# A new order for the 35 DMA transfers of a matmul-and-subtract kernel

## Chip, cores, metric

One core of one Trainium2 chip. The time is device microseconds of one execution; the span in a profile is some 1.8 us shorter than the time of the same run (1.7 to 1.9 us in every run on record). Chips differ little here, but a few runs are up to 3 us longer. Runs over 1.5% above the fastest are called slow and are left out of the verdicts.

The words used below: a transfer is issued when the sync engine's DMA instruction starts, and has landed when its semaphore says that all of its rows are in place. The stream is what the 16 DMA engines move one after another; a hole is a time in which they have nothing queued. The head is the part of the kernel before the steady loop.

## The reference

```python
# x: 16 x 512 x 1024, weight: 1024 x 768, sub_value: 16 x 512 x 768, all float32
def reference(x, weight, sub_value):
    return (np.matmul(x, weight) - sub_value).astype(np.float32)
```

In the kernel, rows are taken in 64 m tiles of 128. Traffic is 33.6 MB of x, 3.1 MB of weight, 25.2 MB of sub_value and 25.2 MB of output: 87.03 MB in all.

## The kernel before

ScalarE casts x to f16. Forty tiles are transposed on TensorE and copied out of PSUM (the memory that TensorE writes) by ScalarE, 24 (in pairs) on VectorE. Each tile then has 16 matmuls of 384 columns. VectorE subtracts, in place in the ring that held sub_value, and the ring's slots are stored. All DMA is issued by the sync engine from one list, in order. An entry is (what, first tile, number of tiles); w counts chunks of 256 rows of the weight:

```python
NX, NSO = 16, 32          # slots of the x ring and of the sub_value/output ring
TRANSFERS = [
    ('x', 0, 1), ('w', 0, 1), ('x', 1, 1), ('w', 1, 1), ('x', 2, 2), ('w', 2, 1),
    ('w', 3, 1), ('x', 4, 4), ('s', 0, 5), ('x', 8, 8), ('s', 5, 3), ('s', 8, 8),
    ...
]
```

An entry waits for what its slots held before; entries behind it wait too (cut from the kernel, comments added):

```python
old = {t - NX if kind == "x" else t - NSO for t in span}
need, by = {
    "w": (set(), "o"),
    "x": ({t for t in old if t >= 0}, "cast"),     # the cast has read the slot
    "s": ({t for t in old if t >= 0}, "o"),        # the store has landed
    "o": (span, "finish"),                         # the subtraction is done
}[kind]
```

The steady loop, cut to its order:

```python
for mi in range(HEAD, n_mt):
    tr = transposes(mi + TA) ...          # unless that pair goes to VectorE
    for c in range(n_c):
        matmuls(mi, c)
        if tr:
            tr[c]()
    ...                                   # casts of later tiles, on ScalarE
    finish(mi)                            # the subtraction, on VectorE
    for f in waiting[:PER]:               # six transpose pieces on VectorE
        f()
```

## Time and profile before

| | kernel before |
|---|---|
| time, first three runs | 211.04 us median (210.6 to 211.05) |
| span of the profiled run | 208.5 us (time of this run 210.34 us) |
| TensorE busy | 195.9 us, 94% |
| DMA queue | 98.0% of 16 engines, 87.03 MB |
| last subtraction ends / last store issued / landed | 203.20 / 203.23 / 207.26 us |

A busy share says that an engine had work, not that it set the end: two rows near 100% can both be read as the bound. The prediction shows the lines. One more line, from the list of DMA issues (size of each, median us from issue to landing), is that of the last two stores:

```profile
out_dram<-so_ring SPq DMA_DIRECT2D x2, 384.0 KB, 4.8
```

A store of 384 KB takes 0.90 us of all engines at their rate; 4.8 us is latency or a queue ahead of it. Which of the two, the profile of this kernel alone doesn't tell.

### The profile page before, as it was taken

To read this page: it belongs to the slowest core of one execution; us is meant where nothing else is said; L and a number is where in the kernel's file an instruction comes from. 1 tells how busy PE (TensorE), PEld (TensorE's weight loads), DVE (VectorE), ACT (ScalarE), POOL (GpSimd) and SP (SyncE) were. 2 spreads that over 40 slices of the span, in tenths; PEclk is the share of its full clock that TensorE was granted. 3 is DMA by queue.
4 is the path that set the end of the run, shared out by engine and by line. 5 is a ranking of instruction groups with operands and counts; after the bars stand their busy time and mean duration, and the time that the engine had idled before them with its cause. 6 is when DMAs were issued, how large, how long until landed. Compare 5 with 4: busy or idle time off the path is not lost.

```text
span 208.5 us, 2449 instructions
## 1 busy us (share of the span) xinstructions
PE 195.9 (94%) x1216; PEld 75.7 (36%) x704; DVE 147.4 (71%) x266; ACT 103.1 (49%) x105; POOL 0.7 (0%) x6
## 2 busy tenths in 40 slices
PE   7959879999999999999999999999999999999970
PEld 2413434443343434343434333343434343344420
DVE  0231043369999999998899969999999999423330
ACT  2640556976446371916463275537291821467400
POOL 1000000000000000000000000000000000000000
PEclk9996999999999999999999999999999999999998
DMA  6999999999999999999999999999999999999994
GB/s 198 424 437 425 458 437 383 457 405 438 433 445 429 439 421 422 442 429 420 408 463 431 417 430 442 445 386 430 434 426 447 424 431 434 443 446 395 460 390 199
DMA packets 4906, 87.17 MB, mean 418 GB/s; under 512 B 544, under 2 KB 544, under 8 KB 1568
## 3 DMA queue, kind: packets, MB, share of 16 engines
q1 hardware_dynamic: 4896, 87.03, 98.0%
q8 instruction: 7, 0.11, 0.2%
q14 instruction: 3, 0.02, 0.0%
HBM read 61.87 MB, written 25.17 MB: 417 GB/s over the span
## 4 chain that ended last, share of the span: by engine, by line
PE 88%; DMA 5%; ACT 1%; SPq 1%; DVE 1%; issue 0%
PE po_b L180 79%; PE pt_b L317 8%; DMA so_ring<-in_weight_dram 5%; ACT xt_b L324 1%; PE po_b L405 1%; SPq L280 1%; DVE w_sb L247 0%; DVE so_ring L388 0%; ACT x_b L299 0%; SPq L244 0%; SPq L517 0%; SPq L134 0%
## 5 line engine op out<-in xcount | busy, mean ns | idle before, releaser
L180 PE MATMUL po_b<-w_sb,xt_b 128*128 128x384 f16 x640 | 113.3, 329 | 3.5 <-DVE w_sb L247 2.6
L344 DVE STREAM_TRANSPOSE xtp_b<-x16p_b 32x256 f32<-32x256 f32 x192 | 83.6, 435 | 8.2 <-ACT x16p_b L299 5.2
L388 DVE TENSOR_TENSOR so_ring<-po_b,so_ring 128x768 f32<-128x768 f32 x64 | 60.0, 956 | 34.7 <-PE po_b L180 21.6
L324 ACT COPY xt_b<-pt_b 128x1024 f16<-128x1024 f16 x40 | 40.4, 1012 | 81.4 <-PE pt_b L317 81.0
L180 PE MATMUL po_b<-w_sb,xtp_b 128*128 128x384 f16 x384 | 73.6, 326 | 0.0
L368 PEld LDWEIGHTS <-xt_b 128*128 128x128 f16 x320 | 31.7, 99 | 63.2 <-issue 60.3
L299 ACT CAST x_b<-x_ring 128x1024 f16<-128x1024 f32 x40 | 41.5, 1045 | 8.8 <-DMA x_ring<-in_x_dram 8.7
L317 PE MATMUL pt_b<-ident,x_b 128*128 128x128 f32 x160 | 41.1, 273 | 1.3 <-ACT x_b L299 1.3
L317 PEld LDWEIGHTS pt_b<-ident,x_b 128*128 128x128 f32 x160 | 22.0, 141 | 34.8 <-issue 31.6
L299 ACT CAST x16p_b<-x_ring 128x1024 f16<-128x1024 f32 x24 | 25.1, 1046 | 3.9 <-DMA x_ring<-in_x_dram 3.8
L368 PEld LDWEIGHTS <-xtp_b 128*128 128x128 f16 x192 | 18.8, 98 | 21.9 <-issue 20.1
L247 DVE CAST w_sb<-so_ring 128x768 f16<-128x768 f32 x8 | 4.1, 557 | 11.8 <-DMA so_ring<-in_weight_dram 11.8
L405 PE MATMUL po_b<-idle_x,idle_w 128*128 128x512 f16 x31 | 9.3, 454 | 1.5 <-DVE idle_x L399 1.5
L405 PEld LDWEIGHTS po_b<-idle_x,idle_w 128*128 128x128 f16 x31 | 3.5, 114 | 5.9 <-issue 2.7
L299 ACT ACT_TABLE_LOAD x1 | 1.3, 1283 | 0.9 <-SPq L134 0.9
L398 DVE MEMSET idle_w<- 128x64 uint32 x1 | 0.1, 112 | 1.0 <-SPq L134 1.0
L418 PE MATMUL po_b<-idle_x,idle_w 128*128 128x512 f16 x1 | 0.4, 379 | 0.0
L169 POOL TENSOR_SCALAR_AFFINE_SELECT ident<-ident 128x128 f32<-128x128 f32 x1 | 0.3, 292 | 0.1
L399 DVE MEMSET idle_x<- 128x256 uint32 x1 | 0.3, 272 | 0.0
L168 POOL MEMSET ident<- 128x128 f32 x1 | 0.2, 206 | 0.5 <-SPq L134 0.5
L418 PEld LDWEIGHTS po_b<-idle_x,idle_w 128*128 128x128 f16 x1 | 0.1, 98 | 0.1
L506 POOL MEMSET const-bfloat16-1.0<- 128x1 bf16 x1 | 0.1, 102 | 0.0
(3 smaller groups left out, 0.3 us busy)
## 6 DMA issues: line engine op xcount, KB each, us to landing
so_ring<-in_sub_value_dram SPq DMA_DIRECT2D x2, 3840.0 KB, 20.1
x_ring<-in_x_dram SPq DMA_DIRECT2D x2, 3584.0 KB, 18.7
x_ring<-in_x_dram SPq DMA_DIRECT2D x2, 3072.0 KB, 23.0
out_dram<-so_ring SPq DMA_DIRECT2D x2, 3072.0 KB, 30.4
out_dram<-so_ring SPq DMA_DIRECT2D x1, 6144.0 KB, 32.9
x_ring<-in_x_dram SPq DMA_DIRECT2D x1, 5120.0 KB, 17.4
so_ring<-in_sub_value_dram SPq DMA_DIRECT2D x2, 2304.0 KB, 16.7
x_ring<-in_x_dram SPq DMA_DIRECT2D x1, 4608.0 KB, 19.7
```

What stands on the lines that cost most here:

```text
L169: pool.add(lambda: nc.gpsimd.affine_select(out=ident, in_=ident, compare_op=mybir.AluOpType.not_equal, fill=1.0, base=0, pattern=[[-1, P]] ...
L180: return nc.tensor.add_instruction(mybir.InstMatmult(name=nc.get_next_instruction_name(), engine=full.engine, ins=list(full.ins), outs=lis ...
L247: lambda at=at, r=r, st=st: nc.vector.tensor_copy(out=w_sb[:, at, r], in_=st[:, r]),
L280: sp.add(lambda here=here, there=there: nc.sync.dma_start(out=here, in_=there), waits, (sem, 16))
L299: act.add(lambda: nc.scalar.copy(out=to, in_=x_in), waits, count("cast"))
L317: pe.add(lambda: nc.tensor.transpose(words, from_, ident), waits, count("turn") if last else None)
L324: act.add(lambda: nc.scalar.copy(out=xt_b[:, d], in_=pt_b[:, b]), waits, count("evac"))
L344: dve.add(lambda: nc.vector.transpose(xt[b * Q : (b + 1) * Q, :, a * Q : (a + 1) * Q], x16[a * Q : (a + 1) * Q, :, b * Q : (b + 1) * Q],), ...
L368: pe.add(lambda weights=weights: nc.tensor.ldweights(weights, tile_position=(0, 0)), [w for w in waits if w[0] in ready])
L388: dve.add(lambda: nc.vector.tensor_tensor(out=o, in0=po[:, :, :NS], in1=o, op=mybir.AluOpType.subtract), [landed["s", mi], (counter["mul"] ...
L405: lambda: nc.tensor.matmul(po_b[:, NPO - 1, 0], idle_w, idle_x, start=True, stop=True),
L418: pe.add(lambda: nc.tensor.matmul(po_b[:, NPO - 1, 0], idle_w, idle_x, start=True, stop=True), [(counter["ident"], 2)])
```

## The change

The intent: the last two weight chunks come ahead of x of the third tile, so that TensorE has no long gap in its head; in the steady part each load is asked for well before it is needed, which takes smaller pieces of x where a slot comes free late (tiles 46 and 48 in pairs).

```diff
-    ('x', 0, 1), ('w', 0, 1), ('x', 1, 1), ('w', 1, 1), ('x', 2, 2), ('w', 2, 1),
-    ('w', 3, 1), ('x', 4, 4), ('s', 0, 5), ('x', 8, 8), ('s', 5, 3), ('s', 8, 8),
-    ('x', 16, 3), ('s', 16, 5), ('x', 19, 6), ('x', 25, 7), ('s', 21, 11), ('o', 0, 8),
-    ('x', 32, 7), ('o', 8, 8), ('s', 32, 6), ('x', 39, 9), ('s', 38, 10), ('x', 48, 10),
-    ('o', 16, 9), ('o', 25, 7), ('s', 48, 6), ('s', 54, 10), ('x', 58, 6), ('o', 32, 16),
-    ('o', 48, 10), ('o', 58, 4), ('o', 62, 1), ('o', 63, 1),
+    ('x', 0, 1), ('w', 0, 1), ('x', 1, 1), ('w', 1, 1), ('w', 2, 1), ('w', 3, 1),
+    ('x', 2, 3), ('s', 0, 5), ('x', 5, 3), ('x', 8, 8), ('s', 5, 3), ('x', 16, 3),
+    ('s', 8, 8), ('x', 19, 7), ('s', 16, 16), ('x', 26, 6), ('x', 32, 6), ('o', 0, 8),
+    ('o', 8, 8), ('s', 32, 7), ('x', 38, 8), ('x', 46, 2), ('s', 39, 9), ('x', 48, 2),
+    ('o', 16, 9), ('x', 50, 8), ('s', 48, 9), ('o', 25, 7), ('x', 58, 6), ('s', 57, 7),
+    ('o', 32, 16), ('o', 48, 10), ('o', 58, 4), ('o', 62, 1), ('o', 63, 1),
```

## The prediction

> **What bounds the kernel now.** I read the page first, for the busy shares, the slices and the chain of work that ended last.
>
> ```profile
> span 208.5 us, 2449 instructions
> PE 195.9 (94%) x1216; PEld 75.7 (36%) x704; DVE 147.4 (71%) x266; ACT 103.1 (49%) x105; POOL 0.7 (0%) x6
> PEclk9996999999999999999999999999999999999998
> DMA  6999999999999999999999999999999999999994
> q1 hardware_dynamic: 4896, 87.03, 98.0%
> PE 88%; DMA 5%; ACT 1%; SPq 1%; DVE 1%; issue 0%
> ```
>
> The chain names TensorE, but the DMA row is at 9 in every slice but the first and last: 16 engines at 98% of the span. So two things may both be the bound. The table by windows settles the DMA side:
>
> ```profile
> core 0: us, PE busy (x) PEld busy (x) DVE busy (x) ACT busy (x) POOL busy (x), PEclk, DMA share, GB/s
> 24.00:44.00 20.00, 18.76 (x123) 8.04 (x74) 7.05 (x9) 14.42 (x16) 0.00 (x0) 1.00 1.01 433
> 104.00:124.00 20.00, 20.00 (x129) 7.45 (x71) 17.75 (x34) 10.48 (x11) 0.00 (x0) 1.00 1.01 436
> 184.00:204.00 20.00, 18.21 (x118) 7.18 (x66) 6.70 (x7) 7.89 (x8) 0.00 (x0) 1.00 0.97 416
> ```
>
> DMA share 1.01 at 433 to 436 GB/s is a full pipe, not a busy-looking one. Next I took each transfer's issue and landing from the trace. The interval between two landings fits MB/0.4352 + 0.073 us to within 0.05 us for nearly all 34 transfers (s of tiles 21 to 31: 4.33 MB, 10.01 us measured, 10.02 by the rule). The 0.073 us is 8 rows per engine at 8 ns plus one semaphore write of 9 ns; packets of 3,072 B take 121 ns and of 49,152 B 1,815 ns, which gives slope and offset. The sum: 87.03/0.4352 = 199.98, and 34 x 0.073 = 2.48, so 202.46 us of pure streaming. The first x (1.28 us of stream) lands at 5.00, so 3.72 us is start and receipt: 206.2. The last store landed at 207.26. Of the missing 1.08 us, 0.80 was lost while x of tiles 8 to 15 passed (a 16 KB instruction fetch ran on one engine at 29.4 us), and the rest in four pieces of 0.05 to 0.25 us. No wait of the program opened a hole in the stream.
>
> Last, the waits and the timeline, for the compute side:
>
> ```profile
> 15.53 4.44 PE L180 MATMUL po_b<-w_sb,xt_b 128*128 128x384 f16 x16 [2.27 <-DVE w_sb L247]
> 25.89 2.69 DVE L388 TENSOR_TENSOR so_ring<-po_b,so_ring 128x768 f32<-128x768 f32 x3 [8.54 <-DMA so_ring<-in_sub_value_dram]
> 28.71 0.33 PE L317 MATMUL pt_b<-ident,x_b 128*128 128x128 f32 x1 [1.00 <-ACT x_b L299]
> 202.25 0.96 DVE so_ring L388
> ```
>
> TensorE has gaps only in the head: 2.27 us for the third weight chunk, then 1.00 us for a cast at 28.71. From 28.71 to 202.25 it runs with no gap worth naming, 3.04 us per tile with TensorE transposes and 2.60 without. It ends at 202.25, the subtraction at 203.21, the last store is issued at 203.23 and lands 4.03 us later. An empty queue took 4.06 us for the first x (issue 0.94, landing 5.00). So the two paths end together within some 0.1 us: TensorE's last tile and the full DMA pipe.
>
> **What the Trainium skill says.** "DMA: Bandwidth & Descriptors", section "Where 436 GB/s comes from", gives 435.2 GB/s as the ceiling of the sixteen ports; this trace's slope is 0.4352 MB/us, in agreement. The same page says that the HBM side binds at about 358 GB/s; with one core alone this trace does not agree. Its section "Queues, rings and completion order" says that each engine consumes descriptors in ring order; the landings here follow issue order throughout. "TensorE: Matmul & The Clock Gate", Part 1, says that the clock halves after a mostly idle 3,413 ns window, free-running. The trace agrees: clock 0.5 from 15.64 to 19.05 us, after TensorE had worked some 1 us of the window before.
>
> **The change part by part.** No compute instruction moves: on TensorE, VectorE, ScalarE and GpSimd the order listing is the same. Only the sync queue's list differs.
>
> (a) One transfer more, 35 instead of 34, same bytes: +0.073 us of streaming. This is the only change to the DMA sum.
>
> (b) Weights ahead of x of tile 2. Landings are 3.72 + MB/0.4352 + 0.073 per transfer. The fourth weight chunk: 4.19 MB, 13.8 us (16.3 before). x of tiles 2 to 4: 5.77 MB, 17.5 (12.5 before for 2 and 3). s of 0 to 4: 7.73 MB, 22.1 (25.8 before). x of 5 to 7: 9.31 MB, 25.75 (21.2 before for 4 to 7). x of 8 to 15: 36.3 if the 0.8 us is lost again, the same as before. The 2.27 us gap at 15.5 shrinks to about 0.5, and with it the half clock, worth 11 matmuls x 0.16 = 1.8 us. But now tile 5's cast waits for 25.75: cast to 26.85, its transposes at 26.9, after a gap of some 2.5 us. Before, the same transposes started at 28.71. So the head gains 1.8 us.
>
> (c) It gives most of that back. Three tiles on, at 26.9 + 3 x 3.04 = 36.0, tile 8's transposes want x that lands at 36.3 and is cast by 37.35: a stall of 1.35. Before, they came at 28.71 + 9.12 = 37.83. So TensorE is 0.4 us ahead.
>
> (d) s of tiles 16 to 31 in one piece lands at about 73.1; before, 16 to 20 landed at 54.67. The subtraction of tile 16 is ready at some 71.8 and waits 1 to 1.3 us. VectorE then does it (0.99), four transpose pieces (4 x 0.45) and tile 17's subtraction (0.96): 76.9. Tile 20 needs that accumulator at about 76.7: up to 0.2 us lost on TensorE.
>
> (e) The steady part. Before, casts of tiles 33 and 41 came late enough to idle VectorE for 1.27 us at 99.6 and 1.77 at 123.3, and the margin between a subtraction and the reuse of its accumulator fell to 0.05 us at tile 40. Earlier x (tiles 46 and 48 in pairs let the casts start sooner) gives about 1.5 us of margin there. It was margin, not a wait: the trace has no more than 0.03 us of TensorE idle at that place. Nothing is gained in time.
>
> Sum: TensorE ends at 202.25 - 0.4 + 0.2 = about 202.05, and would let the last store land at 207.05. The pipe lands it at 207.26 + 0.07 = 207.3. The later one counts. Predicted span 208.6, and with the 2.5 us between the span and the median of 211.04, **211.0 to 211.1**.
>
> **The rivals.** First, the head's gain reaches the end: 1.8 us, 209.2. For it: the chain is 88% TensorE. Against: the pipe is full to the last store and the bytes are the same, so this needs 87 MB at over 438 GB/s, above the slope. Only the hiccups (1.08 us in all) could shrink: 210.2 at best. Second, the new order opens a hole in the pipe: a transfer is issued less than 1.4 us before the one ahead has streamed. s of 32 must wait for the store of 0 to 7 to land (95.0), with the store of 8 to 15 still streaming to 100.9: 4.5 us in hand. s of 57 has as much, the store of 48 to 57 3.8 us, that of 58 to 61 0.7 us. The old order had 2 to 4 us at five such places and 0 at the store of 58, so the new one has more; a hole would be 0 to 1 us, 212. Third, TensorE becomes the later path: the gap before tile 5 falls so that the free-running window halves the clock (up to 1.7 us, of which the stall at tile 8 hides 1.35), or the wait at tile 16 costs 1 us rather than 0.2, since VectorE has only some 0.35 us per four tiles to catch up. Then TensorE ends up to 1 us after 202.25: 211.5 to 212.
>
> **Range and chances.** The three runs before lie between 210.6 and 211.05, so 0.4 us is noise. Below is the floor with no hiccup, 210.2; above, one rival of half a size. So 210.4 to 211.7. Faster by over 2% would be 206.8, below the pipe's floor: 0.01. Slower by over 2% is 215.3, which needs holes of 4 us: 0.02. Within 2%: 0.97.
>
> **What would show it right or wrong.** Right: q1 again at 98% of the span; clock 0.5 gone at 15.6; the cast of tile 5 at 25.8; a gap on TensorE near 37.4 before transposes; a VectorE wait for sub_value ending at 73; TensorE done within 0.5 us of 202.1; last store some 4 us after its issue. Wrong: DMA share below 9 in a middle slice (a hole), TensorE idle for over 0.5 us after 40 us, or a span under 207.5, which would mean that the slope is not a ceiling.

## The result

210.60 us median of six runs (210.31 to 210.68), beside 210.63 us of the kernel before (six runs, 210.17 to 211.05). Ratio 0.9994, 95% interval 0.9978 to 1.0011: the same. A ratio is the mean time of one kernel's fast runs over that of the other's in the same rounds, so not quite the ratio of the medians.

The page of the changed kernel: span, busy time, the slices of clock and DMA, the queue's share, and the chain by engine:

```profile
span 208.5 us, 2452 instructions
PE 194.9 (93%) x1216; PEld 75.2 (36%) x704; DVE 147.3 (71%) x266; ACT 102.4 (49%) x105; POOL 0.7 (0%) x6
PEclk9999999999999999999999999999999999999998
DMA  5999999999999899999999999999999999999994
q1 hardware_dynamic: 5040, 87.03, 97.9%
PE 60%; DMA 31%; DVE 2%; SPq 2%; issue 1%; ACT 1%; DVEq 0%
```

The half clock is gone (the 6 in the fourth slice before is a 9 now), but that isn't the change's doing alone. Later profiles of the same two kernels show it the other way round; here are the clock rows of the changed kernel and then of the kernel before, each taken again:

```profile
PEclk9999969999999999999999999999999999999995
PEclk9999999999999999999999999999999999999995
```

The paragraph on the head, below, says what decides it. The chain went from 88% TensorE to 60%, with loads of x and sub_value in its place, at an unchanged time: the chain follows one of several nearly simultaneous releases, and its shares are no measure of what a change is worth. The DMA row still stands at 9 in all slices but the ends and one, where it is 8. That 8 is no hole: the row, like the tables by windows, counts a packet wholly in the slice in which it starts, and here rows of 49,152 B pass, 1.8 us each. By the packets' own times in the trace the engines are busy for 1.00 of this slice (67.8 to 73.0 us). Shares over 1.00 in the tables come about in the same way.

The table by windows, in the same stretches as before:

```profile
24.00:44.00 20.00, 15.75 (x103) 6.81 (x63) 5.04 (x7) 12.73 (x14) 0.00 (x0) 1.00 1.02 434
104.00:124.00 20.00, 20.00 (x130) 7.42 (x71) 19.46 (x38) 10.75 (x12) 0.00 (x0) 1.00 1.01 434
184.00:204.00 20.00, 18.25 (x119) 7.17 (x66) 6.70 (x7) 7.90 (x8) 0.00 (x0) 1.00 0.98 420
```

In the first, TensorE is idle for 4.25 us where it was idle for 1.24, and the engines of the DMA move as much as before. The timeline shows the two gaps, and VectorE's wait for the large piece of sub_value:

```profile
26.55 0.33 PE L317 MATMUL pt_b<-ident,x_b 128*128 128x128 f32 x1 [2.56 <-ACT x_b L299]
37.58 0.33 PE L317 MATMUL pt_b<-ident,x_b 128*128 128x128 f32 x1 [1.70 <-ACT x_b L299]
73.38 0.96 DVE L388 TENSOR_TENSOR so_ring<-po_b,so_ring 128x768 f32<-128x768 f32 x1 [1.23 <-DMA so_ring<-in_sub_value_dram]
202.28 0.96 DVE so_ring L388
```

The last subtraction starts at 202.28, within 0.03 us of before. The last store is issued at 203.27 and lands at 207.26, as before to the hundredth. So close an agreement is luck: later profiles of the changed kernel have 207.63 and 207.79 us, one of the kernel before 207.71.

### The profile page after: what moved, and what is told of

Its sections match the earlier page's. It is cut to its first block, busy times and chain, and to the rows that moved or that the text cites. A ratio compares the mean times of both kernels' runs of the same rounds, so it can differ in the third digit from the quotient of the medians.

```text
span 208.5 us, 2452 instructions
## 1 busy us (share of the span) xinstructions
PE 194.9 (93%) x1216; PEld 75.2 (36%) x704; DVE 147.3 (71%) x266; ACT 102.4 (49%) x105; POOL 0.7 (0%) x6
## 4 chain that ended last, share of the span: by engine, by line
PE 60%; DMA 31%; DVE 2%; SPq 2%; issue 1%; ACT 1%; DVEq 0%
PE po_b L180 55%; DMA so_ring<-in_sub_value_dram 16%; DMA x_ring<-in_x_dram 15%; PE pt_b L317 5%; DVE so_ring L388 1%; SPq L280 1%; SPq L244 1%; DVE xtp_b L344 1%; ACT xt_b L324 0%; ACT x_b L299 0%; SPq L56 0%; SPq L517 0%; DVEq L56 0%; SPq L134 0%
## 5 line engine op out<-in xcount | busy, mean ns | idle before, releaser
L180 PE MATMUL po_b<-w_sb,xt_b 128*128 128x384 f16 x640 | 111.8, 326 | 0.9 <-DVE w_sb L247 0.6
```

Of the source, the lines that this page charges most:

```text
L180: return nc.tensor.add_instruction(mybir.InstMatmult(name=nc.get_next_instruction_name(), engine=full.engine, ins=list(full.ins), outs=lis ...
```

## The experiments

My theory going in: the DMA engines are full, the bytes are the same, so nothing in the order can shorten the stream; TensorE happens to end beside it. The rival: the chain through TensorE sets the end, and DMA only looks full. Under the rival the time is unchanged because the head's gain was given back at 37.58. The edits were made on the changed kernel.

### A quarter of the matmuls of tiles 40 to 63 left out (wrong result)

From the edit (FULL is 40, n_c is 4; cut: the third chunk's last matmul then closes the sum and counts the tile as done):

```diff
+        if mi >= FULL and c == n_c - 1:
+            return
+        end = n_c - 1 if mi < FULL else n_c - 2
```

> The changed kernel with a quarter of the matmuls of tiles 40 to 63 left out (24 tiles x 4 matmuls x 0.1625 us = 15.6 us of TensorE; wrong result on purpose); transfers untouched. VectorE, 11.1 us per four tiles, will hold TensorE back up to tile 56, so TensorE should end near 194.5 us, some 7.7 us earlier. Pipe theory (the DMA engines are full, TensorE ends beside them): last landing stays at 207.2 to 207.3, span 208.4 to 208.6, time the same within 0.2 us; the last store then takes far longer than 4 us from issue to landing. Rival (the chain through TensorE alone sets the end): 7.7 us faster, span near 201.

Measured: 210.33 us median (four runs, 210.22 to 211.37), ratio 0.9964, 0.9895 to 1.0033; the three runs without the profiled one took 210.22 to 210.43. The DMA issues of the last two stores in its profile:

```profile
out_dram<-so_ring SPq DMA_DIRECT2D x2, 384.0 KB, 13.9
```

The last store was issued at 194.88 us, 8.4 us earlier than in the changed kernel, and waited in the queue for what that gained. (The profiled run, 211.37, was the longest: sub_value of 39 to 47 landed 0.97 us later than its bytes account for; the three others had no such loss in their times.) The chain through TensorE alone is refuted as the bound.

### 2.36 MB of loads left out (wrong result)

```diff
             there = rows(view, at, n)
+            if (kind, at) == ('s', 57):
+                here, there = ring[:, at % size : at % size + 1], rows(view, at, 1)
```

> The changed kernel with the load of sub_value of tiles 57 to 63 cut to tile 57 (six tiles of 0.393 MB less, 2.36 MB, 2.36/0.4352 = 5.4 us of stream; wrong result on purpose); TensorE untouched. Pipe alone: 5.4 us faster, span 203.1. Both paths end together (my theory): TensorE still ends at about 202.2 and the last store still has to be issued at 203.3; only its queueing goes, so 0 to 0.3 us faster, and holes of some 2 to 3 us in the DMA row between 185 and 203.

Measured: 209.04 us (208.59 to 209.14), ratio 0.9888, 0.9823 to 0.9953: about 1.6 us faster than the changed kernel (which did not stand in this set of runs; its medians in three others are 210.50 to 210.88), between the 0 to 0.3 that I expected and the 5.4 of the pipe alone. The table by windows shows where the rest went (second number from the end is the DMA share):

```profile
184.00:188.00 4.00, 4.00 (x28) 1.68 (x15) 0.96 (x1) 2.39 (x3) 0.00 (x0) 1.00 0.55 233
188.00:196.00 8.00, 8.00 (x55) 3.60 (x32) 2.87 (x3) 4.92 (x5) 0.00 (x0) 1.00 1.00 430
196.00:200.00 4.00, 4.00 (x27) 1.46 (x14) 0.96 (x1) 1.01 (x1) 0.00 (x0) 1.00 0.23 98
```

45% of 4 us and 77% of 4 us, 4.9 us by this table and 4.3 us by the packets' own times, stood empty, because the stores of 48 to 57 and 58 to 61 could not be issued before TensorE and VectorE had made their tiles. And the last stores:

```profile
out_dram<-so_ring SPq DMA_DIRECT2D x2, 384.0 KB, 2.8
```

The last was issued at 203.79 and landed at 206.09: 2.30 us, near an empty queue. My expectation rested on 4 us for that. So in the changed kernel, TensorE's path alone would have let the last store land at about 203.27 + 2.30 = 205.57; it landed at 207.26. By this estimate the pipe is the later path by 1.7 us (by 2.2 and 2.3 us in the two later profiles of the changed kernel). The gain of 1.6 us fits it; between the two profiles it is 1.2 us, TensorE's side having ended 0.5 us later in this one.

### Both at once (wrong result)

> Both cuts at once. TensorE ends near 194.5 us, the pipe has 5.4 us less to stream. My theory: the pipe is the later of the two, 207.26 - 5.4 = 201.8 last landing, span 203.1, 5.4 us faster, although neither cut alone gives more than 0.3 us. Chain alone: 7.7 us faster. If neither path were a bound: no change.

Measured: 205.26 us (205.05 to 205.85), ratio 0.9718, 0.9653 to 0.9783. Against the changed kernel's 210.60 that is 5.34 us; the bytes left out are 5.4 us. With TensorE out of the way, bytes turn into time one to one. In the profile the last landing is at 202.28, where 201.8 was expected. The three runs together show the pipe as the bound, with TensorE's path some 1.7 us behind it as the next.

### An early hole in the stream

The two entries, from a longer line of the list:

```diff
-    ('o', 8, 8), ('s', 32, 7),
+    ('s', 32, 7), ('o', 8, 8),
```

> The changed kernel with two entries of the list exchanged: sub_value of 32 to 38, which waits for the store of 0 to 7 to land, now comes before the store of 8 to 15, so nothing is queued behind the store of 0 to 7. Pipe theory: the engines stand empty from the end of that store's stream (93.8) until the next load's first byte: 1.4 us receipt plus 1.4 us issue to first byte = 2.8 us, which no later part can win back: last landing 210.0, span 211.2, 2.7 us slower. TensorE by itself would lose about 1.1 us. Rival (the pipe has slack of its own, its full look is only queueing): under 1.2 us slower.

Measured: 216.06 us (215.82 to 216.14), 5.4 us over the changed kernel; ratio to the kernel before 1.0221, 1.0141 to 1.03, so it is slower, and whether by more than 2% stays unclear. The direction is that of the pipe theory, the size twice the expected one. The table by windows, of this run and then of the changed kernel:

```profile
92.00:97.00 5.00, 5.00 (x34) 1.95 (x19) 4.84 (x10) 2.98 (x4) 0.00 (x0) 1.00 0.48 154
97.00:105.00 8.00, 8.00 (x53) 3.17 (x30) 7.79 (x16) 3.58 (x4) 0.00 (x0) 1.00 0.95 343
105.00:113.00 8.00, 8.00 (x52) 2.70 (x27) 7.79 (x16) 4.79 (x5) 0.00 (x0) 1.00 0.99 425
```

```profile
92.00:97.00 5.00, 5.00 (x34) 1.94 (x19) 4.84 (x10) 2.98 (x4) 0.00 (x0) 1.00 1.01 433
97.00:105.00 8.00, 8.00 (x53) 3.17 (x30) 7.79 (x16) 3.61 (x4) 0.00 (x0) 1.00 0.99 425
105.00:113.00 8.00, 8.00 (x52) 2.72 (x27) 7.79 (x16) 4.79 (x5) 0.00 (x0) 1.00 1.03 444
```

In the 5 us of the hole 5 x (433 - 154)/435 = 3.2 us of stream are missing, in the 8 us after it, with the engines busy again, 8 x (425 - 343)/435 = 1.5 us. After the restart 33 of the 128 rows of 21,504 B took 1.2 to 1.85 us, where in the undisturbed stream they take 0.80. By landings, sub_value of 32 to 38 and the store behind it came 4.06 and 1.50 us later than their bytes account for, 5.56 in all; the engines also ran dry one after another, the first at 92.9 us, the last at 95.0. The expectation had 1.4 us twice in its 2.8; the trace has 0.44 us from the end of the store's last row (94.99) to its landing, and 0.97 us from the next issue (95.45) to the first row (96.42). So the loss is larger through the engines that ran dry early and through the slow rows; why the rows were slow stays open. The compute engines did the same work in these windows. What the stream lost here it never won back. TensorE, which stood still for 3.41 us at 126.49, ended only 4.1 us later than in the changed kernel, the last landing came 5.84 us later: a full pipe has no reserve.

### The parts of the change, and the same kernel again

The changed kernel once more:

> The changed kernel once more, beside the three below on the same chip: ratio to before 0.997 to 1.003.

Measured: 210.50 us (210.26 to 210.68), ratio 0.9983, 0.9957 to 1.001. In its profile the clock was at 0.5 from 27.20 to 30.62 us.

Only the first nine transfers in the new order:

> The first nine transfers in the new order, from x of tile 8 on in the old one (34 transfers). The wait of TensorE for a weight chunk and the half clock go, those at 26.5 and 37.5 for casts come; sub_value of 16 to 20 lands at 54.9 again, so tile 20 does not wait. TensorE ends at about 202.0. Pipe theory: span 208.5 as before, ratio 0.997 to 1.003. Rival (the chain): 0.2 us faster than before.

Measured: 210.89 us (210.4 to 211.47), ratio 1.0003, 0.9974 to 1.0033. TensorE ended at 202.35, not at about 202.0.

Only the rest in the new order:

> The first nine transfers in the old order, from x of tile 8 on in the new one (35 transfers). Half clock at 15.6 and the start of the dense stretch at 28.7 as before; the margin between a subtraction and the reuse of its accumulator at tile 40 is over 1 us, not 0.05. Both theories: ratio 0.997 to 1.003; TensorE ends within 0.2 us of 202.25.

Measured: 210.53 us (210.3 to 210.94), ratio 0.9988, 0.996 to 1.0015. TensorE ended at 202.66 in its profile, 0.4 us after the expected 202.25, and that cost nothing either. The half clock (from 15.29 us) and the margin at tile 40 (1.82 us) are as expected. Within the 0.3% of these intervals, no part has an effect that the other cancels.

### The two points of the head mended

The entries that differ, each side put on one line:

```diff
-    ('x', 8, 8), ('s', 5, 3), ('x', 16, 3), ('s', 8, 8), ('x', 19, 7), ('s', 16, 16),
+    ('x', 8, 2), ('x', 10, 6), ('s', 5, 3), ('s', 8, 8), ('x', 16, 3), ('x', 19, 7), ('s', 16, 5), ('s', 21, 11),
```

> The changed kernel with the two points mended at which it gave its head start back: x of 8 to 15 as 8, 9 and 10 to 15, so that tile 8's cast need not wait for eight tiles; sub_value of 8 to 15 ahead of x of 16; sub_value of 16 to 31 as 16 to 20 and 21 to 31 (37 transfers). TensorE should have no gap after 27 us and end near 200.5, 1.7 us earlier than both kernels. Pipe theory: the bytes are the same and two transfers more cost 2 x 0.073 = 0.15 us, so span 208.5 to 208.7, ratio to before 0.998 to 1.003, and the last store takes some 5.7 us from issue to landing. Rival (the chain through TensorE sets the end): 1.7 us faster, ratio 0.992.

Measured: 210.64 us (210.48 to 210.84), ratio 0.9991, 0.9962 to 1.002. The time is as the pipe theory has it, but the run doesn't test it: TensorE did not end earlier (last store issued at 203.03, not at 201.5). The gap at 37.58 is gone, but after the one before tile 5 the clock was at 0.5 from 26.93 to 30.34 us. The transpose after the gap, and the first matmuls after it, in its timeline:

```profile
26.88 0.46 PE L318 MATMUL pt_b<-ident,x_b 128*128 128x128 f32 x1 [2.56 <-ACT x_b L300]
27.14 1.49 PE L181 MATMUL po_b<-w_sb,xt_b 128*128 128x384 f16 x4
```

Four matmuls take 1.49 us from first start to last end, 0.81 us in the kernel before at 28.88. The gap is 2.56 us in both kernels; whether it costs the clock is a matter of where the clock's window falls: in the changed kernel's first profile it did not, in its two later ones it did (from 27.20 and 27.54 us). So the test needed a filled gap, here with matmuls on zeros that wait for the subtraction of tile 2:

```diff
+            if mi == HEAD and c == 0:
+                for _ in range(9):
+                    pe.add(lambda: nc.tensor.matmul(po_b[:, NPO - 1, 0], idle_w, idle_x, start=True, stop=True), [(counter["finish"], HEAD)])
             if tr:
                 tr[c]()
```

> The order of the run that mended both points, plus nine matmuls on zeros in the 2.56 us gap of TensorE before tile 5 (they wait for the subtraction of tile 2), so that no window of the clock falls mostly idle there: in the profile of the mended order without them the clock was 0.5 from 26.93 to 30.34 us, which ate the head's gain again (TensorE ended as late as in the changed kernel, last store issued at 203.03). Expected: clock 1.0 from 6 us to the end, TensorE ends near 200.5, last store issued near 201.6, some 1.6 us before that of both kernels. Pipe theory: last landing at 207.3 to 207.5 all the same, ratio to before 0.997 to 1.002. Rival (the chain through TensorE): 1.6 us faster, 0.992.

Measured: 210.68 us (five runs, 210.59 to 211.11), ratio 1.0001, 0.9985 to 1.0017. The clock was 1.0 from 6.28 to 204.25 us. Last subtraction, DMA row and the last two stores in its profile:

```profile
200.73 0.96 DVE L389 TENSOR_TENSOR so_ring<-po_b,so_ring 128x768 f32<-128x768 f32 x1 [1.64 <-PE po_b L181]
DMA  6999999999999999999999999999999999999994
out_dram<-so_ring SPq DMA_DIRECT2D x2, 384.0 KB, 6.7
```

TensorE and VectorE end 1.55 us earlier than in the changed kernel. The last store is issued at 201.72 and lands at 207.58; the last two are 6.7 us under way instead of 4.8. The whole gain of the compute side ends up as waiting in the queue. This version, correct and with all the head's gain kept, is no faster than either kernel: an order that lets TensorE end earlier wins nothing. What an order could still change is the loss in the stream itself, some 1 to 2 us against bytes over rate; no run tried that.

### Spread

In the runs so far, the kernel before had shown some long times and the changed one none. Both once more, on the same chip as the last run:

> The kernel before, submitted as a run of its own. So far 6 of 30 runs with the old order from tile 8 on took over 211.4 us (up to 213.58), none of 24 with the new order. Theory (spread): the old order has transfers with under 4 us in hand which now and then come late; then about one run in five here is over 211.4 us. Rival (those runs belonged to the chips and the moment): the rate is the same in the next run.

Measured: 211.07 us (210.33 to 211.95), two of six over 211.4 us.

> The changed kernel, submitted a third time, interleaved with the two others. Theory (spread): none of its runs over 211.4 us, median 210.3 to 210.7. Rival: as many as in the run before.

Measured: 210.88 us (210.43 to 211.08), ratio 1.0004, 0.999 to 1.0019, none over 211.4 us; the median is over the expected 210.3 to 210.7. The runs of the kernel before that stood beside them (eleven, 210.4 to 211.4) had none either, so the set by itself decides nothing. Over all sets, 8 of 47 runs with the old order from tile 8 on took over 211.4 us (one of them slow by the rule above), and none of 35 with the new one, whose longest took 211.11. The limit of 211.4 us was chosen after the first of these had been seen, and no profile fell in a long run, so what makes a run long, and that asking early prevents it, stays open.

## Why the prediction was right

**The bound and the size.** "The pipe lands it at 207.26 + 0.07 = 207.3": it landed at 207.26, where the better start of the stream (first landing at 4.69 us instead of 5.00) made up for part of a greater loss at x of tiles 8 to 15 (1.32 us instead of 0.80), and smaller losses elsewhere for the rest; that the sum came out to the hundredth is luck. That the pipe is the bound was argued from rate and bytes; the run with less TensorE work, the run with both cuts and the run with the filled gap have shown it. The predicted 211.0 to 211.1 us is still 0.4 to 0.5 us too long: the span was right (208.6 predicted, 208.5 measured), but the 2.5 us added to it set the span of one run beside the median of three others. That run took 210.34 us, which makes the difference 1.8, and 208.6 + 1.8 = 210.4.

**One step was wrong.** "So the two paths end together within some 0.1 us": they don't. I took the 4.06 us of the very first load, of whose 128 rows 29 ran slowly (0.2 to 1.0 us each instead of 0.16), for the latency of an empty queue. At the end of a run it is 2.30 us. TensorE's path has 1.7 us in hand, which the run with fewer bytes turned into 1.6 us of time. The error did not reach the predicted time, since the later path counts, but it made the third rival's 211.5 to 212 too long: with 1.7 us in hand, a slip of 1 us on TensorE's side would not have been seen in the time at all.

**The head.** Expected: a gap of some 2.5 us ending at 26.9, a stall of 1.35 us before 37.4. Measured: 2.56 us ending at 26.55, 1.70 us ending at 37.58; the stall is longer because x of 8 to 15 landed at 36.46. TensorE was then 0.30 us ahead (37.88 in the kernel before), not 0.4.

The half clock at 15.6 (15.63 to 19.05 us in the kernel before) is gone, as expected, but the gap alone doesn't decide that. In all 13 profiles the clock changes only at whole steps of 3.41 us from its first change, and these steps lie elsewhere in each run. TensorE's idle time summed over each step from the traces separates the cases: after every step at full clock with 2.11 us of idle time or more the clock was at 0.5, after none with 1.95 us or less. The same gap of 2.27 us near 15.5 lay within one step in the first profile of the kernel before and was cut by a step's end in its second (1.95 us in the fuller step), which shows no half clock. The gap of 2.56 us before tile 5 was cut in the first profile of the changed kernel (1.84 us in the fuller step) and lay within one step in its two later ones (2.55 and 2.57 us), where the clock halved, as in four other profiles of its variants. Even the stand of 3.41 us at 126.49 in the run with the hole, cut into two steps with 1.61 and 1.81 us, did not halve it. So the half clock at the new gap, which the prediction named only under the rivals, came in 6 of the 9 profiles that have this gap; in the two later ones of the changed kernel TensorE ended at 202.1 to 202.2 us all the same, because the half clock then took the place of the stall at 37.58.

**Tile 16's wait.** Expected: sub_value landing at 73.1 and up to 0.2 us lost on TensorE. Measured: 73.29, VectorE idle for 1.23 us, and tiles 18 and 19 take 2.71 and 2.81 us from start to start instead of 2.60: 0.3 us. TensorE's side then ends at 202.28, 0.2 us later than expected.

**The steady part.** The margin between a subtraction and the reuse of its accumulator at tile 40 rose from 0.05 to 1.82 us (about 1.5 expected), with no gain in time, as expected: it was margin and not a wait.

**Holes.** None opened in the new order; the sign "DMA share below 9 in a middle slice" was met by the one 8, but falsely, as shown under the result. "A hole would be 0 to 1 us, 212" speaks of a transfer issued a little late. None was seen, so this stays untested; the hole made on purpose, with the next issue after the landing, cost 5.4 us for 2.8 of worked-out idle time. The "0 at the store of 58" of the old order is not in the trace: that store was issued at 197.92 us, at 197.96 in the new order, and its landing fits bytes over rate to 0.05 us in both.

## What to carry to other kernels

Before reordering transfers, lay bytes over rate plus the cost of each transfer beside the landings. If every interval fits, as nearly all did here, the order has little to give and fewer bytes help until the next path binds (5.4 us less of stream gave 1.6 us here), and an engine at 94% with the chain pointing at it may still have time in hand. How much shows in the last store: compare its time from issue to landing with that on an empty queue at the same place, not with the first load of the run. Keep something queued at all times: where a load had to restart the stream, its rows ran slowly on top of the time in which the engines stood empty. (Where stores restarted it, in the run with fewer loads, their rows took 0.46 to 0.50 and 1.14 to 1.18 us, hardly over the usual 0.46 and 1.14.) And take more than one profile of each kernel before crediting a change with a clock that comes or goes.

## What the Trainium skill lacked or had wrong

- "DMA: Bandwidth & Descriptors", "Where 436 GB/s comes from", has the HBM side bind at about 358 GB/s for transfers between HBM and SBUF, and the prediction took this as a disagreement. The sentence lacks its condition, which the same page gives under "Measured": with both cores of an HBM domain streaming, each gets about 358 GB/s. With one core running, loads and stores ran here at 435 GB/s for 200 us on end.
- The same page, "Latency and other measured facts", gives about 600 ns to the first byte for a transfer issued by hardware, without saying from when. In the hole, the load issued at 95.45 us moved its first row at 96.42: 0.97 us from the start of the issuing instruction, 0.64 us from its end. Counted from the end, the page and the trace agree.
- "TensorE: Matmul & The Clock Gate", Part 1, has the clock halve after an idle window of about 3.4 us. The step of 3.41 us is there in the traces, but 2.11 us of idle time within one were enough, and 1.95 us were not.
- No page that I read gives the price of a restart: after the hole, rows of 21,504 B took up to 1.85 us instead of 0.80, 1.5 us of stream on top of 3.2 us missing in the hole.
- "Runtime: NRT & Kernel Launch", "Instruction fetch mechanics", puts the cost of crossing a 16 KiB block of instructions at one DMA tail-bump, mostly hidden; what the fetch takes from a full stream of data it doesn't say. Each profile shows seven rows of 16,384 B, of 0.9 to 1.1 us each. While the first passed, x of tiles 8 to 15 (or 8 and 9) came 0.7 to 1.6 us late in all profiles; while the six others passed, at most 0.14 us was lost in the first profiles of the two kernels. So that the fetch is the cause of the 0.7 to 1.6 us is not shown, and the six others speak against it.
